# Layer 1 of a two-layer decoder trunk: the order of five engines taken from a list scheduler in the kernel's source, in place of the framework's order on four of them

## The chip, the cores and the metric

The kernel runs on one core of one Trainium2 chip. The metric is the device time of one execution in microseconds, as the median of several runs. One profiled execution gives the trace from which all other figures come.

## What is computed

A trunk of two layers over 1024 tokens of width 1024, batch 1. Layer 0 mixes by gated causal pooling; then one K/V pair is made from the stream; layer 1 is attention with 16 query heads on 2 shared K/V heads, in a window of 128 tokens, with a bias by distance and a sink per head. The part that the change touches, cut from the reference:

```python
kb, vb = shared_kv_blocks(x, c_act, ...)     # rmsnorm, modulate, x @ w_kv, banded blocks
h = modulate(rmsnorm(x, norm_g[l]), shift, scale)
q, z = jnp.split(h @ w_in, 2, axis=-1)
s = jnp.einsum('bqhgd,bkhd->bhgqk', qn, kn) + pos_bias
s = jnp.where(mn, s, NEG_INF)
m = jnp.maximum(jnp.max(s, axis=-1, keepdims=True), sink)
p = jnp.exp(s - m)
p = p / (jnp.sum(p, axis=-1, keepdims=True) + jnp.exp(sink - m))
o = jnp.einsum('bhgqk,bkhd->bqhgd', p, vn)
y = (o * jax.nn.silu(z)) @ w_out
x = x + gate[:, None, :] * y
return rmsnorm(x, final_g)
```

## The kernel before

Activations lie transposed: channels on the 128 partitions, tokens along the free axis. The stream is eight tiles `xk[n]` of 128 channels x 1024 tokens. The 1024 tokens are worked in two halves of 512, q=0 and q=1. Every matrix product is made of three passes of half precision each (fp32r): high times high, high times low, low times high. So every operand exists as a high part and a low part: ScalarE (ACT) casts the high part, VectorE (DVE) subtracts it from the value to get the low part. A **dense step** is the three matmuls of one slice of 128 channels (L200 to L202), and a dense tile has eight of them, or four for a tile of the output product.

Layer 1 (L1022 to L1414, from about 603 us on) is a list `specs` of pieces, worked one after the other: for each half and each group r of four heads a `project` (two tiles of queries L1085, two of gates L1102); keys and values of the second half (L1047, L1063); the output product in parts (`out_part` L1199, and in quarters of 256 tokens at the very end, `out_quarter` L1222); the norms' statistics and the final norm (`finish` L1277). Pieces marked `bare` only start other work and add 0.1 to the clock.

Between the steps of these pieces run the **attention blocks** (`attend` L1119), one per head group and block of 128 tokens, 32 in all. A block's chain crosses four engines: PE makes the scores (L1138, L1139, tile ps_S); DVE masks (L1140) and takes row maxima (L1144); ACT takes four exponentials (L1148, tile pt); DVE the reciprocal (L1151) and the division pt (L1152); PE transposes pt (L1158, tile ps_tp); ACT and DVE split that into high and low (L1161, L1162); POOL masks it with two selects (L1167, L1170); PE multiplies with the values (L1181, L1182, tile ps_o); ACT and DVE add, gate and split the result into qt (L1184 to L1194). `LAGS`, `GAPS` and `FIRST` date the blocks' three pieces on PE, in a clock that counts only dense steps (KSTEP, L1038).

`Modulated` (L924) makes the normed and modulated input of a product, tile hm: DVE makes xn from x (L937), ACT adds the shift and casts the high part (L939), DVE takes the low part (L943). hk1 is the input of the second half's keys and values, h11 that of its queries and gates; `prepare` (L1348) dates their eight steps each.

**Weights.** `load_any` (L1251) fetches a weight two pieces ahead and splits it in the same place of the program. A weight that the first half has split already comes back from memory on POOL's queue (L1262, tiles kw). A new one is loaded on SP's queue into raw1, of which there are two (L1265), cast by ACT (L1266) and split by DVE (L1267), and its two parts are stored to memory by SP (`keep`, L147). The four last output weights (tile wo) stay on the chip and are not stored.

**What sets the order.** Only PE's instructions are issued in the order written (`manual_schedule`, L1401). The order of ACT, DVE, POOL and SP comes from the framework's own scheduler, which sees the same program.

Of the kernel before, what the change touches and what calls it, by code (L numbers as in the profile page):

```python
# [59 lines left out]
def trunk(ctx, tc, xT, c, pack, ada_first, ada_rest, wu0_in, wg0_in, wa, wg, wao, wkv,  # L60
# [976 lines left out]

    KSTEP = 3 * 0.2133  # L1038

    def gemm_steps(w, off, acts, n, done, cols=H):  # L1040
        ps = bank("d")[:, :cols]
        for k in range(n):
            dense_mm(ps, w, off, acts, k, n)
            yield KSTEP * cols / H
        done(ps)

    def keys(q, hk, ps=None):  # L1047
        def done(ps):
            cols = half(q)
            for kv in range(2):  # L1050
                a, b = slice(kv * 64, kv * 64 + 64), slice((1 - kv) * 64, (1 - kv) * 64 + 64)
                nc.scalar.copy(out=KH[kv][a, cols], in_=ps[a, :])
                nc.scalar.copy(out=KH[kv][b, cols], in_=ps[a, :])
                hs = KH[kv][a, cols].bitcast(F32)
                nc.vector.tensor_sub(out=KL[kv][a, cols], in0=ps[a, :], in1=hs)
                nc.vector.tensor_sub(out=KL[kv][b, cols], in0=ps[a, :], in1=hs)
# [6 lines left out]
    def values(q, hk, ps=None):  # L1063
        def done(ps):
            vts[q] = bp.tile([P, H], F32, tag="ol", name="vt", bufs=1)
            nc.scalar.copy(out=vts[q], in_=ps)
# [4 lines left out]
    def values_split(q):  # L1071
        def run(w):
            ps = bank("d")
            for j in range(4):
                nc.tensor.transpose(ps[:, j * P:(j + 1) * P], vts[q][:, j * P:(j + 1) * P], ident)
            pv = ps.rearrange("p (s c) -> p s c", c=64)
            vh, vl = VS[:, q * 8:q * 8 + 8, 0, :], VS[:, q * 8:q * 8 + 8, 1, :]
            nc.scalar.copy(out=vh, in_=pv)
            nc.vector.tensor_sub(out=vl, in0=pv, in1=vh.bitcast(F32))
# [5 lines left out]
    def queries(q, r, j, h1):  # L1085
        def run(w):
            if j == 0:
                pool, tag, bufs = (bp, "q2", 2) if r < 2 else (hp, "h", 8)
                qts[q, r] = pool.tile([P, 2, 2, H], F32R, tag=tag, name="qt", bufs=bufs)
            qt = qts[q, r]  # L1090

            def done(ps):
                for e in range(2):
                    a, b = slice(e * 64, e * 64 + 64), slice((1 - e) * 64, (1 - e) * 64 + 64)
                    nc.scalar.activation(qt[a, j, e, :], ps[a, :], AF.Copy, scale=0.125)
                    nc.vector.scalar_tensor_tensor(
                        out=qt[b, j, e, :], in0=ps[a, :], scalar=0.125,
                        in1=qt[a, j, e, :].bitcast(F32), op0=ALU.mult, op1=ALU.subtract)
# [3 lines left out]
    def gates(q, r, j, h1):  # L1102
        def run(w):
            if j == 0:
                szs[q, r, "tile"] = bp.tile([P, 2, H], F32, tag="szb", name="szb", bufs=2)
            sz = szs[q, r, "tile"]

            def done(ps):
                nc.scalar.activation(sz[:, j, :], ps, AF.Tanh, scale=0.5)
                nc.vector.scalar_tensor_tensor(out=sz[:, j, :], in0=sz[:, j, :], scalar=1.0,  # L1110
                                               in1=ps, op0=ALU.add, op1=ALU.mult)
# [7 lines left out]
    def attend(q, r, b):  # L1119
        kv = r // 2  # L1120
        qt = qts[q, r]
        cols = slice((b % 4) * P, (b % 4) * P + P)


        pt = bp.tile([P, 4, P + 8], F32, tag="P", name="pt", bufs=2)
        nc.gpsimd.tensor_copy(out=pt[:, :, P:P + 1],
                              in_=nsink[:, 4 * r:4 * r + 4].unsqueeze(2))
        nm = sp.tile([P, 4], F32, tag="nm", name="nm")
        den = sp.tile([P, 4], F32, tag="den", name="den")
        for j in range(2):  # L1130
            s = bank("S").rearrange("p (e c) -> p e c", e=2)
            lo = 0 if b else P
            if b == 0:
                nc.vector.memset(s[:, :, :P], NEG)
            for e in range(2):
                lhs = qt[:, j, e, cols]
                ks = slice((b - 1) * P + lo, (b + 1) * P)
                mm(s[:, e, lo:], lhs, KH[kv][:, ks], start=True, stop=False)  # L1138
                mm(s[:, e, lo:], lhs, KL[kv][:, ks], start=False, stop=True)  # L1139
            nc.vector.copy_predicated(out=s[:, :, :P], mask=tri, data=s[:, :, P:])  # L1140
            for e in range(2):
                i = 2 * j + e
                hd = 4 * r + i
                nc.vector.tensor_tensor_reduce(  # L1144
                    out=pt[:, i, :P], in0=s[:, e, :P], in1=bias[:, hd, :],
                    scale=-1.0, scalar=nsink[:, hd:hd + 1], op0=ALU.add, op1=ALU.min,
                    accum_out=nm[:, i:i + 1])
                nc.scalar.activation(pt[:, i, :P + 1], pt[:, i, :P + 1], AF.Exp,  # L1148
                                     bias=nm[:, i:i + 1], scale=-1.0,
                                     accum_out=den[:, i:i + 1])  # L1150
        nc.vector.reciprocal(out=den, in_=den)  # L1151
        nc.vector.tensor_mul(out=pt[:, :, :P], in0=pt[:, :, :P],  # L1152
                             in1=den.unsqueeze(2).broadcast_to([P, 4, P]))
        yield LAGS[0]
        tp = bank("tp")
        for j in range(2):
            for e in range(2):
                nc.tensor.transpose(tp[:, (e * 2 + j) * P:(e * 2 + j + 1) * P],  # L1158
                                    pt[:, 2 * j + e, :P], ident)
# [310 lines left out]
```

## Time and profile before

| | us |
|---|---|
| median of three runs | 984.7 (983.31 to 985.41) |
| the profiled execution, its own time | 985.74 |
| its span (first to last instruction in the trace) | 983.9 |
| granted TensorE clock, mean of the span | 0.992 |

| engine | busy us | share | instructions |
|---|---|---|---|
| PE (matmul) | 964.3 | 98% | 4538 |
| DVE | 748.7 | 76% | 1405 |
| ACT | 421.5 | 43% | 860 |
| POOL | 152.9 | 16% | 238 |

The span lies 1.84 us below the execution's own time. A row of the trace's timeline has the start, the length, the engine, the line, the operation, the tiles (out<-in) and, in brackets, how long the engine had stood idle before it and what ended that idle time. PE's matmuls overlap, so the distance from one start to the next, not the length, is what one costs.

### The profile page before, as it was taken

How to read it: one execution, taken by the hardware profiler on the slowest of the kernel's cores; microseconds unless marked ns; L12 is line 12 of the kernel's file. 1: busy time of each engine (PE TensorE's matmuls, PEld its weight loads, DVE VectorE, ACT ScalarE, POOL GpSimd, SP SyncE). 2: the span in 40 equal slices, each digit the busy share in tenths (PEclk: the TensorE clock that was granted, in tenths of full speed). 3: DMA queues.
4: the chain of work that ended last, by engine and by line, in shares of the span. 5: the costliest groups of instructions: out<-in, count | busy, mean ns of one | idle time of the engine just before them, and what ended most of it. 6: DMA issues, size and time to landing. Idle time of an engine off the chain costs nothing.

```text
span 983.9 us, 12776 instructions
## 1 busy us (share of the span) xinstructions
PE 964.3 (98%) x4538; PEld 804.2 (82%) x4538; DVE 748.7 (76%) x1405; ACT 421.5 (43%) x860; POOL 152.9 (16%) x238
## 2 busy tenths in 40 slices
PE   8999999999999999999999999999999999999996
PEld 6788888888888888888888888887888888887896
DVE  5897978686977799676765478498999666777684
ACT  5534434332433344551122245355665434454434
POOL 3100000000000000000022101231313433443523
PEclk9999999999999999999999999999999999999998
DMA  9452621254225411788878726745556454353022
GB/s 337 167 183 107 203 97 65 76 202 150 65 81 197 150 64 57 258 280 307 303 277 276 273 65 225 275 138 182 207 207 221 130 171 141 131 185 101 1 87 86
DMA packets 51570, 165.53 MB, mean 168 GB/s; under 512 B 5681, under 2 KB 7857, under 8 KB 51378
## 3 DMA queue, kind: packets, MB, share of 16 engines
q1 hardware_dynamic: 39120, 119.10, 34.8%
q0 software_dynamic: 12240, 44.57, 13.4%
q10 hardware_dynamic: 146, 1.05, 0.4%
q8 instruction: 35, 0.57, 0.2%
q14 instruction: 29, 0.24, 0.1%
HBM read 128.00 MB, written 36.70 MB: 167 GB/s over the span
## 4 chain that ended last, share of the span: by engine, by line
PE 80%; DVE 14%; ACT 2%; issue 2%; DMA 1%; POOL 1%; POOLq 0%; DVEq 0%; SPq 0%; ACTq 0%
PE ps_d L211 14%; PE ps_S L211 9%; PE ps_d L633 9%; PE ps_d L200 7%; PE ps_d L201 7%; PE ps_d L202 7%; PE ps_S L633 4%; PE ps_o L211 4%; PE ps_tp L211 3%; PE ps_d L371 2%; PE ps_o L633 2%; PE ps_tp L633 2%; DVE tmp L539 2%; PE ps_tp L1158 1%; PE ps_S L1139 1%
## 5 line engine op out<-in xcount | busy, mean ns | idle before, releaser
L201 PE MATMUL ps_d<-hm,w 128*128 128x512 f32 x264 | 103.4, 392 | 1.9 <-DVE hm L943 1.9
L200 PE MATMUL ps_d<-hm,w 128*128 128x512 f32 x264 | 104.7, 397 | 0.0
L202 PE MATMUL ps_d<-hm,w 128*128 128x512 f32 x264 | 103.4, 392 | 0.0
L236 DVE CUSTOM_DVE_ANT_0 tmp<-tmp,cact,pk 128x1024 f32<-128x1024 f32 x48 | 60.7, 1282 | 28.2 <-DMA tmp<-ada_rest 27.9
L211 PE MATMUL ps_d<-gh,wh 128*128 128x512 f32 x224 | 81.9, 389 | 0.0
L1148 ACT ACTIVATE pt<-pt,nm 128x129 f32<-128x129 f32 x128 | 50.2, 395 | 36.9 <-DVE nm L1144 33.0
L211 PE MATMUL ps_S<-gh,wh 128*128 128x512 f32 x192 | 64.5, 390 | 0.0
L633 PE MATMUL ps_d<-hs,ws 128*128 128x512 f32 x264 | 63.4, 389 | 0.0
L201 PEld LDWEIGHTS ps_d<-hm,w 128*128 128x128 f32 x264 | 49.8, 189 | 11.4 <-DVE hm L943 2.3
L202 PEld LDWEIGHTS ps_d<-hm,w 128*128 128x128 f32 x264 | 49.7, 188 | 11.1 <-DMA w<-kw 0.4
L633 PEld LDWEIGHTS ps_d<-hs,ws 128*128 128x128 f32 x264 | 49.6, 188 | 10.3
L200 PEld LDWEIGHTS ps_d<-hm,w 128*128 128x128 f32 x264 | 49.8, 189 | 9.2
L539 DVE TENSOR_TENSOR tmp<-tmp 128x1039 f32<-128x1039 f32 (+3 forms) x40 | 49.4, 1234 | 6.8 <-ACT tmp L669 5.8
L531 POOL MEMSET tmp<- 128x16 f32 x16 | 1.7, 112 | 331.4 <-DVE tmp L539 117.9
L633 PE MATMUL ps_d<-ha,ws 128*128 128x512 f32 x216 | 51.9, 389 | 0.0
L126 ACT CAST wh<-raw 128x1024 fp32r<-128x1024 f32 x28 | 29.4, 1050 | 49.4 <-PE ps_d L211 33.9
L609 ACT CAST ws<-tw 128x512 fp32r<-128x512 f32 x44 | 26.7, 621 | 53.7 <-PE ps_tp L211 15.1
L211 PEld LDWEIGHTS ps_d<-gh,wh 128*128 128x128 f32 x224 | 42.0, 188 | 8.8
L633 PEld LDWEIGHTS ps_d<-ha,ws 128*128 128x128 f32 x216 | 40.6, 188 | 8.4
L1262 POOL DMA_DIRECT2D w<-kw x58 | 31.5, 544 | 85.1 <-PE ps_d L202 44.5
L211 PE MATMUL ps_d<-gh,wl 128*128 128x512 f32 x112 | 43.6, 389 | 0.0
L1188 DVE SCALAR_TENSOR_TENSOR of<-ps_o,ol 64x256 f32<-64x256 f32 x64 | 26.6, 416 | 20.9 <-ACT ol L1184 20.2
(308 smaller groups left out, 2569.6 us busy)
## 6 DMA issues: line engine op xcount, KB each, us to landing
w<-kw POOLq DMA_DIRECT2D x58, 512.0 KB, 4.2
tmp<-ada_rest SPq DMA_DIRECT2D x42, 512.0 KB, 4.8
raw<-wa SPq DMA_DIRECT2D x28, 512.0 KB, 3.5
kw<-w SPq DMA_DIRECT2D x24, 512.0 KB, 2.8
raw<-wao SPq DMA_DIRECT2D x20, 512.0 KB, 5.3
ad<-ada_first SPq DMA_DIRECT2D x16, 512.0 KB, 4.7
x<-xT SPq DMA_DIRECT2D x32, 256.0 KB, 5.9
kept_g<-tmp SPq DMA_DIRECT2D x14, 512.0 KB, 2.9
```

The costliest lines, as they stand in the source:

```text
L126: nc.scalar.copy(out=wh, in_=raw)
L200: mm(ps, lh, acts(k, 0), start=k == 0, stop=False)
L201: mm(ps, lh, acts(k, 1), start=False, stop=False)
L202: mm(ps, ll, acts(k, 0), start=False, stop=k == n - 1)
L211: mm(p, lhs, acts(k, hl, q), start=start and k == 0 and s == 0, stop=stop and k == n - 1 and s == 2)
L236: nc.vector.tensor_tensor_reduce(out=raw, in0=raw, in1=ca, scale=0.5, scalar=pk[:, bcol:bcol + 1], op0=ALU.mult, op1=ALU.add, accum_out=ad ...
L539: nc.vector.tensor_add(out=nx[:, 2 * s - 1:], in0=cur[:, 2 * s - 1:], in1=cur[:, s - 1:PAD + T - s])
L609: nc.scalar.copy(out=ws[i][:, 0, :], in_=src)
L633: mm(ps, lhs, acts(k, hl), start=start and k == 0 and s == 0, stop=k == 3 and s == 2, skip_group_check=True)
L1148: nc.scalar.activation(pt[:, i, :P + 1], pt[:, i, :P + 1], AF.Exp, bias=nm[:, i:i + 1], scale=-1.0, accum_out=den[:, i:i + 1])
L1188: nc.vector.scalar_tensor_tensor(out=of[e * 64:(e + 1) * 64, :], in0=o[0:64, es], scalar=0.5, in1=ol[0:64, es], op0=ALU.mult, op1=ALU.add)
L1262: nc.gpsimd.dma_start(dst, src)
```

## The change

No operation of layer 1 is added or taken away (`Modulated` becomes `Second` there, with the same three operations per step). What changes is who decides the order. Every operation is first noted with its engine, a length in us estimated by the author, and the tiles (and parts of tiles) that it reads and writes. Objects `Buf` stand for tiles that are not yet allocated, with the ring of buffers that each takes its turn in. `in_order` then plans. PE's notes keep the order in which they are written. Each gets a wanted time from the lengths ahead of it on PE. The notes of the other engines get theirs backward from those who need them. Then a simulated run takes, at each step, the engine that can begin earliest, and on it the ready note with the smallest wanted time. All notes are issued in the order of their planned beginnings, under a manual schedule of all five engines (PE, ACT, DVE, POOL, SP).

Beside that, `load_any` is parted in two: `fetch_any` issues the load two pieces ahead, `split_any` takes the cast, the split and the stores one piece ahead. Three added `bare` entries hand large buffers on, and each adds 0.1 to the clock of the blocks.

The diff, cut to its core:

```diff
     KSTEP = 3 * 0.2133
+    class Buf:
+        def __init__(self, make, ring=None, turns=0):
+            self.make, self.tile, self.touched, self.parts = make, None, [], {}
...
+    LAG = {PE: 0.25, ACT: 0.15, DVE: 0.12, POOL: 0.12, SP: 0.0}
+
+    def note(engine, length, f, reads=(), writes=(), lag=None):
...
+    def in_order():
...
+            if n.engine == PE:
+                n.want = t
+                t += n.length
+        for n in reversed(notes):
+            if n.engine != PE:
+                n.want = min([t + 12.0] + [
+                    m.want if n in m.follows and n not in m.needs
+                    else m.want - n.length - n.lag for m in n.next])
...
+                if some:
+                    begin = max(free[e], min(n.ready for n in some))
+                    n = min((n for n in some if n.ready <= begin),
+                            key=lambda n: (n.want, number[n]))
+                    if best is None or begin < best[0]:
+                        best = begin, n
...
+        return sorted(notes, key=lambda n: (n.begin, number[n]))
...
+        note(PE, 0.69 if cols == H else 0.365, f,
+             w[0].on + w[1].on + a[0].on + a[1].on, [(ps, 0)])
...
-                nc.scalar.activation(pt[:, i, :P + 1], pt[:, i, :P + 1], AF.Exp,
-                                     bias=nm[:, i:i + 1], scale=-1.0,
-                                     accum_out=den[:, i:i + 1])
-        nc.vector.reciprocal(out=den, in_=den)
...
+            note(ACT, 0.41, lambda: nc.scalar.activation(
+                pt()[:, i, :P + 1], pt()[:, i, :P + 1], AF.Exp, bias=nm()[:, i:i + 1],
+                scale=-1.0, accum_out=den()[:, i:i + 1]),
+                [(nm, i), (pt, "sink")], [(pt, i), (den, i)])
...
+        note(DVE, 0.66, lambda: nc.vector.tensor_mul(
+            out=pt()[:, :, :P], in0=pt()[:, :, :P],
+            in1=den().unsqueeze(2).broadcast_to([P, 4, P])),
+            [(den, i) for i in rows], [(pt, i) for i in rows])
...
-    def load_any(key):
...
+    def fetch_any(key):
...
+                note(POOL, 0.55, lambda: nc.gpsimd.dma_start(w[i](), kept_w[key][i]),
+                     kept_at[key][i].on if key in kept_at else (), w[i].on, 5.0)
...
+        raw = tile_of("raw1", bp, [P, 1024], F32, 2)
+        src = (wb if key[0] == "b" else wbo)[key[1:]]
+        note(SP, 0.35, lambda: nc.sync.dma_start(raw(), src), (), [(raw, 0)], 3.6)
+        return key, raw, None
+
+    def split_any(key, raw, w):
...
+        note(ACT, 1.0, lambda: nc.scalar.copy(out=w[0](), in_=raw()), [(raw, 0)], w[0].on)
+        note(DVE, 1.16, lambda: nc.vector.tensor_sub(
+            out=w[1](), in0=raw(), in1=w[0]().bitcast(F32)), [(raw, 0)] + w[0].on, w[1].on)
...
+                note(SP, 0.35, lambda: nc.sync.dma_start(kept_w[key][i], w[i]().bitcast(F32)),
+                     w[i].on, kept_at[key][i].on, 4.0)
...
-    hk1 = Modulated(1, None, 8, 48)
-    h11 = Modulated(1, None, 16, 24)
...
+            note(DVE, 0.68, lambda: nc.vector.scalar_tensor_tensor(
+                out=f(), in0=xk[k][:, half(1)], scalar=a, in1=rb(), op0=ALU.mult, op1=ALU.mult),
+                x_on(k, 1) + [(rb, 0)], [(f, 0)])
...
+    hk1, h11 = Second(8, 48), Second(16, 24)
...
-        keys(1, hk1), values(1, hk1),
+        keys(1, hk1), values(1, hk1), bare(lambda: large.extend(hk1.tiles)),
...
-    with tc.manual_schedule(engines={mybir.EngineType.PE}):
...
+    loaded = {srcs[0]: [whole(rings[t][1]) for t in ("wh", "wl")]}
+    asked = [fetch_any(specs[i][0]) for i in srcs[1:2]]
...
+                loaded[srcs[nxt]] = split_any(*asked.pop(0))
+            if nxt + 1 < len(srcs):
+                asked.append(fetch_any(specs[srcs[nxt + 1]][0]))
...
+    with tc.manual_schedule(engines=set(LAG)):
+        for n in in_order():
+            n.f()
```

**ScalarE at the last output weights.** These are the rows of ACT around the third and fourth of the weights that stay (wo), where the third block of the last head group is under way. In the program before (cur is the high part of the transposed block, szb the gate, ol and qt the block's result):

```order
L1161 CAST cur<-ps_tp 128x512
L1184 ACTIVATE ol<-ps_o 64x512
L1266 CAST wo<-raw_7576 128x1024
L1193 CAST qt<-of 128x2x128
L1148 ACTIVATE pt,den<-pt,nm 128x129 x2
L1109 ACTIVATE szb<-ps_d 128x512
L1266 CAST wo<-raw_7664 128x1024
L1148 ACTIVATE pt,den<-pt,nm 128x129 x2
L1184 ACTIVATE ol<-ps_o 64x512
```

and the same place now (P is the tile that was called pt, ph that of cur):

```order
L1364 CAST ph<-ps_tp 128x512
L1397 ACTIVATE ol<-ps_o 64x512
L1341 ACTIVATE P,den<-P,nm 128x129 x4
L1288 ACTIVATE szb<-ps_d 128x512
L1413 CAST qt<-of 128x2x128
L1534 CAST wo<-raw_7452 128x1024
L1534 CAST wo<-raw_7471 128x1024
```

Of the two casts of wo that stood between and ahead of the exponentials, both now follow them, behind the gate and the block's qt.

**VectorE at the eighth tile of hk1.** These are the rows of DVE ahead of the eighth low part of hk1 (hm). Before, from the gating of one block to the division of the next:

```order
L1144 ISA pt,nm<-ps_S,bias,nsink 128x128
L1144 ISA nm 128x1
L1110 SCALAR_TENSOR_TENSOR szb<-szb,ps_d 128x512
L1267 TENSOR_TENSOR w_5308<-raw_5309,w_5307 128x1024
L1151 RECIPROCAL den<-den 128x4
L943 SCALAR_TENSOR_TENSOR hm<-xn,adac,hm 128x512
L1152 TENSOR_TENSOR pt<-pt,den 128x4x128
```

and now, from the division of the block ahead, which the three last hm of hk1 follow:

```order
L1350 TENSOR_TENSOR P<-P,den 128x4x128
L1660 SCALAR_TENSOR_TENSOR hm<-xn,adac,hm 128x512 x3
L1410 TENSOR_TENSOR of<-of,szb 128x256
L1321 MEMSET ps_S 128x2x128
L1290 SCALAR_TENSOR_TENSOR szb<-szb,ps_d 128x512
L1415 TENSOR_TENSOR q_4850<-of,q_4850 128x2x128
L1654 SCALAR_TENSOR_TENSOR xn<-x,acol,rb_5035 128x512
L1403 SCALAR_TENSOR_TENSOR of<-ps_o,ol 64x256
L1365 TENSOR_TENSOR ph<-ps_tp,ph 128x512
L1330 COPY_PREDICATED ps_S<-tri,ps_S 128x2x128 x2
L1403 SCALAR_TENSOR_TENSOR of<-ps_o,ol 64x256
```

The eighth hm stood behind the maxima, a gate (szb) and the split of the first new weight. It now stands ahead of the gate and of all that the next block needs (the maxima follow the last row shown, and that split follows the maxima).

**SyncE between the loads and stores of new weights.** The rows of SP for the first of them, before (raw is the tile loaded, kw the copy in memory):

```order
L1265 DMA raw_5356<-wb 128x1024
L147 DMA kw<-w_5307 128x1024
L147 DMA kw<-w_5308 128x1024
L1265 DMA raw_5440<-wb 128x1024
L147 DMA kw<-w_5354 128x1024
L147 DMA kw<-w_5355 128x1024
```

and now (raw, wh and wl behind kw<- are the names that the two split parts have there):

```order
L1518 DMA raw_4804<-wb 128x1024
L1542 DMA kw<-raw 128x1024
L1518 DMA raw_5362<-wb 128x1024
L1542 DMA kw<-raw 128x1024
L1542 DMA kw<-wh 128x1024
L1518 DMA raw_5414<-wb 128x1024
L1542 DMA kw<-wl 128x1024
```

The next load stood behind both stores of a weight; it now stands between the two.

More of the change, by code (lines that the diff above doesn't have):

```diff
@@ L1038, in trunk, with __call__ @@
     KSTEP = 3 * 0.2133
+    PE, ACT, DVE, POOL, SP = ET.PE, ET.Activation, ET.DVE, ET.Pool, ET.SP
+    notes, touched = [], {}
+    class Buf:
+        def __init__(self, make, ring=None, turns=0):
+            self.make, self.tile, self.touched, self.parts = make, None, [], {}
+            self.old = self.before = None
+            if ring is not None:
+                self.old = ring[-turns] if len(ring) >= turns else None
+                self.before = ring[-1] if ring else None
+                ring.append(self)
+        def __call__(self):
+            if self.tile is None:
+                self.tile = self.make()
+            return self.tile
@@ new lines, in trunk, with there, ring_of, tile_of @@
+    rings = {}
+    def there(tile):
+        return Buf(lambda: tile)
+    def ring_of(name, *tiles):
+        rings[name] = [there(t) for t in tiles]
+    def tile_of(name, pool, shape, dtype, bufs):
+        return Buf(lambda: pool.tile(shape, dtype, tag=name, name=name, bufs=bufs),
+                   rings.setdefault(name, []), bufs)
+    large = [Buf(lambda t=t: t) for t in (*hk0.tiles, *h10.tiles)]
+    first_tiles, large = large[4:], large[:4]
+    def large_tile(shape, name):
+        t = Buf(lambda: hp.tile(shape, F32R, tag="h", name=name))
+        t.old = large.pop(0)
+        return t
@@ L1121, in attend @@
         qt = qts[q, r]
[L1122 to L1131, printed above, removed]
+        c = b % 4
+        cols = slice(c * P, c * P + P)
@@ new lines, in attend, with scores @@
+        pt = tile_of("P", bp, [P, 4, P + 8], F32, 2)
+        nm, den = [tile_of(t, sp, [P, 4], F32, 2) for t in ("nm", "den")]
+        note(POOL, 0.25, lambda: nc.gpsimd.tensor_copy(
+            out=pt()[:, :, P:P + 1], in_=nsink[:, 4 * r:4 * r + 4].unsqueeze(2)),
+            (), [(pt, "sink")])
+        ks = slice((b - 1) * P if b else 0, (b + 1) * P)
+        k_on = [(t, (h, x)) for t in (KHb[kv], KLb[kv]) for h in range(2)
+                for x in sorted({max(b - 1, 0) // 4, b // 4})]
+        def scores(j):
+            bk = bank_of("S")
+            s = lambda: bk().rearrange("p (e c) -> p e c", e=2)
@@ L1151, in attend @@
-        nc.vector.reciprocal(out=den, in_=den)
-        nc.vector.tensor_mul(out=pt[:, :, :P], in0=pt[:, :, :P],
-                             in1=den.unsqueeze(2).broadcast_to([P, 4, P]))
-        yield LAGS[0]
[L1155 to L1159, printed above, removed]
-        cur = bp.tile([P, 2, H], F32R, tag="ph", name="cur", bufs=2)
@@ L1211, in out_part @@
+            for i in range(2):
+                yield from tile(i, 2 * n2 + i)
         return ("o", part, n2), run
@@ new lines, in split_any, with note_stats, sums, f @@
+        return w
+    def note_stats(sq, n, more=None):
+        st = bank_of("o")
+        v, rs = [tile_of(t, sp, [P, 8], F32, 2) for t in ("v", "rs")]
+        parts = (sq,) if more is None else (sq, more)
+        def sums(i, t):
+            def f():
+                for j in range(n):
+                    mm(st()[:, j:j + 1], t()[:, j * P:(j + 1) * P], invd,
+                       start=i == 0 and j == 0, stop=j == n - 1 and i == len(parts) - 1)
+            note(PE, 0.15 * n, f, t.on, [(st, 0)])
+        for i, t in enumerate(parts):
+            sums(i, t)
+        note(DVE, 0.2, lambda: nc.vector.tensor_scalar_add(
+            out=v()[:, :n], in0=st()[:, :n], scalar1=EPS), [(st, 0)], [(v, 0)])
+        note(POOL, 1.0, lambda: nc.gpsimd.tensor_tensor(
+            out=rs()[:, :n], in0=v()[:, :n], in1=mhalf[:, :n], op=ALU.pow), [(v, 0)], [(rs, 0)])
+        state["rs"] = rs
@@ L1389, in trunk @@
         *project(1, 2, h11, GAPS[6]),
[L1390 removed]
+        *project(1, 3, h11, GAPS[7]), bare(lambda: large.extend(h11.tiles)),
         *project_out(1, 0)[:2],
```

497 lines of the change are left out of this document (350 added, 147 removed).

## The prediction

> **What bounds the kernel now.** I read the page first (busy times and the chain), then who waited for whom on the matrix engine from 570 us on, then the timeline at each wait that this names, and last the busy times by stretch.
>
> ```profile
> span 983.9 us, 12776 instructions
> PE 964.3 (98%) x4538; PEld 804.2 (82%) x4538; DVE 748.7 (76%) x1405; ACT 421.5 (43%) x860; POOL 152.9 (16%) x238
> PE 80%; DVE 14%; ACT 2%; issue 2%; DMA 1%; POOL 1%; POOLq 0%; DVEq 0%; SPq 0%; ACTq 0%
> ```
>
> TensorE (PE) is busy for 964.3 of 983.9 us, and the chain that ended last is mostly PE. The change removes no matmul. So all it can win is time in which PE stands still or runs slowly while layer 1 is computed (from about 603 us on). The waits view of PE from 570 us lists all of it (total, times, longest):
>
> ```profile
> PE ps_tp L1158 <- DVE pt L1152: 3.4, 5, 2.0
> PE ps_d L201 <- DVE hm L943: 1.9, 1, 1.9
> PE ps_tp L173 <- POOL rs L166: 1.1, 1, 1.1
> PE ps_o L161 <- DVE sqq L1243: 0.6, 1, 0.6
> PE ps_o L161 <- ACT sqq L1241: 0.2, 1, 0.2
> ```
>
> The last three lie behind the last big matmul (973 us) and belong to the closing chain of the norm. The first two are six stalls in the middle; the timeline of PE gives them one by one (start, length, then in brackets the idle time before it):
>
> ```profile
> 664.45 0.63 PE L1158 MATMUL ps_tp<-ident,pt 128*128 128x128 f32 x4 [0.24 <-DVE pt L1152]
> 673.63 0.50 PE L201 MATMUL ps_d<-hm,w 128*128 128x512 f32 x1 [1.91 <-DVE hm L943]
> 687.78 0.63 PE L1158 MATMUL ps_tp<-ident,pt 128*128 128x128 f32 x4 [0.17 <-DVE pt L1152]
> 734.84 0.63 PE L1158 MATMUL ps_tp<-ident,pt 128*128 128x128 f32 x4 [0.52 <-DVE pt L1152]
> 744.61 0.63 PE L1158 MATMUL ps_tp<-ident,pt 128*128 128x128 f32 x4 [0.45 <-DVE pt L1152]
> 892.90 0.74 PE L1158 MATMUL ps_tp<-ident,pt 128*128 128x128 f32 x4 [1.97 <-DVE pt L1152]
> ```
>
> They sum to 5.3 us. The stretches (busy us of PE, PEld, DVE, ACT, POOL with counts, then the granted clock, DMA share, GB/s) show what else they cost, and who is short of time:
>
> ```profile
> 640.00:660.00 20.00, 20.00 (x102) 16.86 (x101) 19.70 (x43) 12.48 (x26) 6.50 (x10) 1.00 0.34 113
> 660.00:670.00 10.00, 9.76 (x50) 7.96 (x49) 9.72 (x27) 5.44 (x14) 3.36 (x5) 1.00 0.38 116
> 670.00:680.00 10.00, 8.09 (x34) 6.32 (x33) 9.36 (x22) 5.54 (x15) 1.18 (x2) 0.83 0.74 258
> 680.00:760.00 80.00, 78.86 (x395) 65.86 (x395) 74.32 (x192) 49.76 (x125) 18.41 (x22) 1.00 0.56 204
> 760.00:880.00 120.00, 120.00 (x599) 101.35 (x598) 80.62 (x238) 53.73 (x163) 48.10 (x70) 1.00 0.45 149
> 890.00:900.00 10.00, 8.03 (x35) 6.65 (x34) 7.58 (x22) 4.09 (x16) 3.67 (x5) 0.83 0.15 47
> 900.00:973.00 73.00, 73.00 (x452) 65.53 (x451) 52.35 (x128) 34.22 (x88) 28.92 (x29) 1.00 0.13 48
> ```
>
> Two things are to be seen. Behind each of the two long stalls the granted clock is 0.83 over 10 us, so 10 x 0.17 = 1.7 us more are lost each time; the four short ones (0.17 to 0.52) leave it at 1.00. And from 640 to 760 us VectorE (DVE) is busy for 113 of 120 us: there it is nearly the bound, and the order of its work decides whether PE's piece is ready. After 760 us it has a third of its time free (80.6 of 120).
>
> The Trainium skill (TensorE: Matmul & The Clock Gate, HAM oscillation) says that PE falls to half clock after idle gaps of more than about 3.4 us. This trace differs: gaps of 1.91 and 1.97 us already brought it. By that rule both stalls would cost their idle time alone, and what there is to win would be 3.4 us less; the measured clock decides.
>
> **The ceiling.** 5.3 us of idle and 2 x 1.7 us of clock make 8.7 us. PE's starts show a little more, since a stalled matmul also loses the overlap with its neighbour (0.1 to 0.16 us at each of six): 9.5 us at most.
>
> **Part 1, ScalarE's written order at the last weights (the stall at 892.90).** The rows of the transfer queue, ScalarE (ACT) and VectorE that lead to it:
>
> ```profile
> 881.90 1.69 SPq L1265 DMA_DIRECT2D raw<-wbo  x2
> 886.36 1.05 ACT L1266 CAST wo<-raw 128x1024 fp32r<-128x1024 f32 x1 [3.28 <-DMA raw<-wbo]
> 887.62 0.40 ACT L1148 ACTIVATE pt<-pt,nm 128x129 f32<-128x129 f32 x1
> 889.02 1.04 ACT L1266 CAST wo<-raw 128x1024 fp32r<-128x1024 f32 x1
> 890.35 0.39 ACT L1148 ACTIVATE pt<-pt,nm 128x129 f32<-128x129 f32 x1
> 890.96 1.19 DVE L1267 TENSOR_TENSOR wo<-raw,wo 128x1024 fp32r<-128x1024 f32 x1
> 892.07 0.69 DVE L1152 TENSOR_TENSOR pt<-pt,den 128x512 f32<-128x512 f32 x1
> ```
>
> ACT stood for 3.28 us at the cast of the third output weight, whose transfer was still under way; the four exponentials of the block stood behind it, two of them even behind the fourth cast, and on DVE the fourth split (1.19) stood between the reciprocal and the division pt. In the new rows all four exponentials stand ahead of the third cast, and DVE's reciprocal and division are neighbours. Without the cast ahead of them the exponentials follow their maxima, so the last ends more than 2 us sooner. 1.97 + 1.7 = 3.7 us go. What is late next there is nothing that I can find: the third and fourth weight are used two output tiles later, and their casts (2 x 1.05) and splits (2 x 1.19) fit before the next block's maxima, as before.
>
> **Part 2, VectorE's order ahead of the second-half keys (the stall at 673.63).** PE waits for the low half of the eighth modulated tile of hk1. DVE's rows:
>
> ```profile
> 664.81 1.99 DVE L937 SCALAR_TENSOR_TENSOR xn<-x,acol,rb 128x512 f32<-128x512 f32 x3
> 671.04 0.68 DVE L1110 SCALAR_TENSOR_TENSOR szb<-szb,ps_d 128x512 f32<-128x512 f32 x1
> 671.64 1.21 DVE L1267 TENSOR_TENSOR w<-raw,w 128x1024 fp32r<-128x1024 f32 x1
> 672.86 0.71 DVE L943 SCALAR_TENSOR_TENSOR hm<-xn,adac,hm 128x512 fp32r<-128x512 f32 x1
> 673.50 0.68 DVE L1152 TENSOR_TENSOR pt<-pt,den 128x512 f32<-128x512 f32 x1
> ```
>
> What PE needs next of these, from its timeline (the transposes of that division, and the first step with h11):
>
> ```profile
> 677.93 0.75 PE L1158 MATMUL ps_tp<-ident,pt 128*128 128x128 f32 x4
> 781.77 0.48 PE L200 MATMUL ps_d<-hm,w 128*128 128x512 f32 x1
> ```
>
> At 664.81 DVE began tiles of xn that only h11 needs (used from 781.77 us on), and just ahead of the wanted hm it evacuated a gate and split a weight that comes a whole weight tile later: 0.68 + 1.21 us at the head of the queue. In the new rows the eighth hm stands one attention block earlier, ahead of that block's maxima. The work moved behind it (one gate, one split, one xn) is wanted later than the keys. 1.91 + 1.7 = 3.6 us go. DVE is full here, so the price is that something else is later; the nearest is the division pt of the same block, done at 674.2 and wanted at 677.93 in the old order, some 3.6 us sooner once the stall is gone. I count nothing for it, between 0 and the 0.52 of the next short stall.
>
> **Part 3, the four short stalls (0.24 + 0.17 + 0.52 + 0.45 = 1.4 us).** All are the division pt, late behind other DVE work. The new order puts reciprocal and division next to each other in every block, but often an hm, a split or evacuations just ahead of them, where the exponentials leave a hole. Bounds: 1.4 us won, or 1.4 us and as much again lost, because with the two long stalls gone PE arrives up to 7 us sooner at the same full DVE; but h11's work can wait until 781.77 us, and DVE has some 6 us unused between 640 and 760. I take 0.
>
> **Part 4, what moves without a price.** SP now issues the next raw load between the two stores of a split weight, 0.3 to 0.4 us earlier; only that second store waits behind it, and nobody reads it for tens of us. POOL's row is nearly the same. Three added steps of the program, each 0.1 on the clock by which the attention blocks are dated, shift some blocks by one step of three matmuls on PE; nothing is added. Waits of split weights come one weight later in the program, but the same rings (raw1 x2, three pairs) free them at the same matmuls. In the closing chain all five rows are the same, so its time stays:
>
> ```profile
> 975.64 0.70 POOL L166 TENSOR_TENSOR rs<-v,mhalf 128x2 f32<-128x2 f32 x1 [1.26 <-DVE v L164]
> 977.65 2.74 DVE L1295 TENSOR_TENSOR x<-x,ps_tp 128x256 f32<-128x256 f32 x8 [2.09 <-PE ps_tp L173]
> ```
>
> **The sum.** 3.7 + 3.6 + 0 = 7.3 us. The profiled execution took 985.74 us, 1.84 beyond its span; it would come to 978.4. The median of the three runs, 984.7, lies 1.0 below it: **977.4 us**.
>
> **The rivals.** One: only the ACT stall goes, and VectorE stays late from 640 to 760. For it: 113 of 120 us busy, and a plan with one length per operation meets operations whose length varies:
>
> ```profile
> L1152 DVE TENSOR_TENSOR pt<-pt,den x32: 668/692/1504, 630.6 to 938.5; 128x512 f32<-128x512 f32 x32
> DMA to landing us min/median/max: 3.8/4.4/14.1
> ```
>
> (the first is the division, shortest, median, longest; the second is the raw loads of L1265). The plan gives the division 0.66 us. Against it: the eighth hm is moved by a whole block, far more than 0.8. Time: 984.7 - 3.7 = 981.0. The Trainium skill (SBUF — State Buffer, Who interferes with whom) says that a VectorE instruction with two SBUF inputs contends with a GpSimd instruction that reads SBUF. The division of 1.50 us began while a select of POOL ran, so the trace agrees; a plan that knows only engines would meet this at random.
>
> Two, it does not do what it says: each stall that goes comes back elsewhere in the same full stretch, and a new cast or split stands in front of another block: 984.7.
>
> Three, slower: the weight casts. The plan counts 0.35 + 3.6 us from issue to landing, the trace's median is 4.4 and the longest 14.1. Sixteen fresh weights come through here, and each cast now has a fixed place in ACT's row with exponentials behind it. A cast that waits as the one at 886.36 did costs 3.7 us. Two of them undo the gain, from the third on it is slower: 977.4 + 3 x 3.7 = 988.5. Against it: in the old order, also fixed, only one of sixteen waited, and the load is now issued no later.
>
> **How the numbers follow.** Forecast 0.66, rival one 0.15, two 0.08, three 0.11. This kernel's measurement tells 0.2% (2 us) from no change. The forecast and rival one are faster: 0.81; rival two is the same: 0.08; three is slower: 0.11. The forecast's own range is 975.2 (the 9.5 us ceiling) to 979.5 (short stalls lose another 1.4 and some); taking in rival one with 2 us for a stall that comes back gives 975.0 to 983.0, which leaves out rivals two and three, 0.19.
>
> **What would show it.** In the new profile: no PE wait for hm (L1660) and no ACT wait for a raw output weight ahead of exponentials; granted clock 1.00 in every 10 us from 640 to 970; PE's waits for the division under 1.5 us in total; a closing chain of the same 10 to 11 us. Wrong if PE waits anew for a weight, a modulated tile or an exponential by more than 2 us in one place, or if the clock falls again.

## The result, and the profile after

| | before | after |
|---|---|---|
| median, us (6 runs each) | 985.06 (983.31 to 986.08) | 975.49 (975.02 to 977.02) |
| the profiled execution / its span, us | 985.74 / 983.9 | 977.02 / 975.3 |
| PE waits from 570 us to the last big matmul, us | 5.3, six stalls | 0.65, one |

The ratio is 0.9909 (95% interval 0.9896 to 0.9922), some 9 us. The prediction was 977.4, within 975.0 to 983.0; the result lies 1.9 us below the forecast, near the lower end. The profiled execution after is the slowest of its six. The page and the waits of PE from 570 us on (total, times, longest):

```profile
span 975.3 us, 12806 instructions
PE 961.7 (99%) x4538; PEld 803.7 (82%) x4538; DVE 751.3 (77%) x1405; ACT 421.1 (43%) x860; POOL 149.4 (15%) x238
```

```profile
PE ps_tp L1574 <- POOL rs L1564: 1.1, 1, 1.1
PE ps_tp L1360 <- DVE P L1350: 0.6, 1, 0.6
PE ps_o L1557 <- DVE ol L1487: 0.6, 1, 0.6
PE ps_o L1557 <- ACT ol L1484: 0.2, 1, 0.2
```

The wait for hm is gone, and of five waits for the division one is left; the other three rows are the closing chain. The same stretches as before (busy us of PE, PEld, DVE, ACT, POOL, then the granted clock):

```profile
640.00:660.00 20.00, 20.00 (x101) 16.86 (x101) 18.90 (x43) 12.44 (x30) 5.47 (x9) 1.00 0.40 135
660.00:670.00 10.00, 10.00 (x52) 8.40 (x51) 9.75 (x27) 5.83 (x16) 4.51 (x7) 1.00 0.43 148
670.00:680.00 10.00, 10.00 (x52) 8.42 (x51) 9.92 (x29) 7.93 (x22) 1.55 (x2) 1.00 0.68 195
680.00:760.00 80.00, 79.35 (x402) 66.77 (x401) 77.28 (x191) 49.90 (x126) 18.11 (x23) 1.00 0.64 221
890.00:900.00 10.00, 10.00 (x51) 8.47 (x50) 7.43 (x25) 5.48 (x20) 5.58 (x8) 1.00 0.31 105
```

The clock is 1.00 in all of them. VectorE is busier than before: 18.90 + 9.75 + 9.92 + 77.28 = 115.9 of 120 us, against 113.1. It does its work with one wait of PE left, of 0.65 us. The two old places, from DVE's and PE's timelines, first the eighth hm, then the division of the block at the third kept weight:

```profile
662.53 0.69 DVE L1350 TENSOR_TENSOR P<-P,den 128x512 f32<-128x512 f32 x1
663.14 2.07 DVE L1660 SCALAR_TENSOR_TENSOR hm<-xn,adac,hm 128x512 fp32r<-128x512 f32 x3
672.19 0.39 PE L1191 MATMUL ps_d<-hm,wh 128*128 128x512 f32 x1
882.92 0.69 DVE L1350 TENSOR_TENSOR P<-P,den 128x512 f32<-128x512 f32 x1
886.78 0.60 PE L1360 MATMUL ps_tp<-ident,P 128*128 128x128 f32 x4
```

The eighth hm is done at 665.2 and wanted at 672.19, by the second matmul of the eighth step; the division is done at 883.6 and wanted at 886.78.

**The account of the profiled pair.** These are starts of PE and its stretch of the chain that ends layer 0, before and after, and the last big matmul:

```profile
589.48 10.88 PE ps_S L211 x48
973.02 0.28 PE L202 MATMUL ps_d<-qt,wo 128*128 128x256 f32 x1
```

```profile
590.67 10.88 PE ps_S L211 x48
965.31 0.28 PE L1192 MATMUL ps_d<-qt,wo 128*128 128x256 f32 x1
```

Layer 0, in which no instruction differs, took 1.2 us more. Layer 1 went from 383.54 to 374.64, 8.9 us less. The closing chain went from 983.9 - 973.02 = 10.9 to 975.3 - 965.31 = 10.0. That makes 1.2 - 8.9 - 0.9 = -8.6, the difference of the spans.

To price each stall I summed what PE's starts lie apart beyond the usual pitch (227 ns for a matmul of 512 columns, 120 for 256, 109 for 128); this takes in the idle time, the half clock behind it and the lost overlap. Before: 3.81 us around 673.63, 3.74 around 892.90, and 0.35 + 0.37 + 0.71 + 0.60 = 2.03 at the four short stalls. After: 0.76 at the one that is left (712.83). That is 3.81 + 3.74 + 2.03 - 0.76 = 8.8 us, against the 8.9 that layer 1 became shorter.

### The profile page after: what moved, and what is told of

Same layout as the page of the kernel before. It is cut to its first block, busy times and chain, and to the rows that moved or that the text cites. A ratio compares the mean times of both kernels' runs of the same rounds, so it can differ in the third digit from the quotient of the medians.

```text
span 975.3 us, 12806 instructions
## 1 busy us (share of the span) xinstructions
PE 961.7 (99%) x4538; PEld 803.7 (82%) x4538; DVE 751.3 (77%) x1405; ACT 421.1 (43%) x860; POOL 149.4 (15%) x238
## 4 chain that ended last, share of the span: by engine, by line
PE 86%; DVE 10%; issue 2%; DMA 1%; POOL 1%; ACT 1%; POOLq 0%; SPq 0%; DVEq 0%; ACTq 0%
PE ps_d L211 14%; PE ps_S L211 9%; PE ps_d L633 9%; PE ps_d L1190 7%; PE ps_d L1192 7%; PE ps_d L1191 7%; PE ps_S L633 4%; PE ps_o L211 4%; PE ps_tp L211 3%; PE ps_d L371 2%; PE ps_o L633 2%; PE ps_tp L633 2%; DVE tmp L539 2%; PE ps_d L304 2%; PE ps_S L304 1%
## 5 line engine op out<-in xcount | busy, mean ns | idle before, releaser
L1341 ACT ACTIVATE P<-P,nm 128x129 f32<-128x129 f32 x128 | 50.2, 394 | 46.7 <-DVE nm L1337 46.5
L1190 PE MATMUL ps_d<-hm,wh 128*128 128x512 f32 x176 | 69.5, 395 | 0.0
L1191 PE MATMUL ps_d<-hm,wh 128*128 128x512 f32 x176 | 68.7, 390 | 0.0
L1192 PE MATMUL ps_d<-hm,wl 128*128 128x512 f32 x176 | 68.6, 390 | 0.0
L211 PEld LDWEIGHTS ps_S<-gh,wh 128*128 128x128 f32 x192 | 35.9, 188 | 7.4
L1372 POOL TENSOR_SCALAR_AFFINE_SELECT pp<-ph 128x1024 fp32r<-128x1024 f32 x28 | 30.8, 1098 | 57.9 <-DVE ph L1365 57.8
L128 DVE TENSOR_TENSOR wl<-raw,wh 128x1024 fp32r<-128x1024 f32 x28 | 34.2, 1221 | 6.6 <-ACT wh L126 5.2
L1192 PEld LDWEIGHTS ps_d<-hm,wl 128*128 128x128 f32 x176 | 33.0, 188 | 7.1
```

What stands on the lines that cost most here:

```text
L128: nc.vector.tensor_sub(out=wl, in0=raw, in1=wh.bitcast(F32))
L211: mm(p, lhs, acts(k, hl, q), start=start and k == 0 and s == 0, stop=stop and k == n - 1 and s == 2)
L1190: mm(p, lh, a[0](), start=k == 0, stop=False)
L1191: mm(p, lh, a[1](), start=False, stop=False)
L1192: mm(p, ll, a[0](), start=False, stop=k == n - 1)
L1341: note(ACT, 0.41, lambda: nc.scalar.activation(pt()[:, i, :P + 1], pt()[:, i, :P + 1], AF.Exp, bias=nm()[:, i:i + 1], scale=-1.0, accum_ou ...
```

## The experiments

Each kernel was run beside the kernel before, so the ratio to it (95% interval) is what compares them: the changed kernel has 0.9909.

**All but the plan.** The notes are issued in the order noted, only PE's order is fixed. PE's instructions stand exactly as in the changed kernel.

```diff
-    with tc.manual_schedule(engines=set(LAG)):
-        for n in in_order():
+    with tc.manual_schedule(engines={PE}):
+        for n in notes:
```

> The changed kernel without the planner: all notes are issued as noted, with PE's order exactly as in the changed kernel, and the order of ScalarE, VectorE, GpSimd and SyncE left to the framework as before. Loads two weights ahead, splits one ahead, and the three added steps of 0.1 stay. Theory (the planned order of the other engines is the whole gain): 983 to 985, with the two long stalls back at the eighth hm and at the third kept weight. Rival (the splitting one weight later, or the shift of attention blocks on PE by a step, is what removed the stalls): 975 to 977.

986.29 us, ratio 1.0011 (0.9996 to 1.0026): the whole gain is gone. The stalls of PE in this kernel's timeline:

```profile
688.12 0.63 PE L1360 MATMUL ps_tp<-ident,P 128*128 128x128 f32 x4 [2.28 <-DVE P L1350]
718.07 0.63 PE L1360 MATMUL ps_tp<-ident,P 128*128 128x128 f32 x4 [2.17 <-DVE P L1350]
894.40 0.63 PE L1360 MATMUL ps_tp<-ident,P 128*128 128x128 f32 x4 [1.27 <-DVE P L1350]
```

The last is at the old place, the block of the third kept weight. At the other old place, the eighth hm, PE waits 0.70 us (at 673.42). The two longest stalls, of over 2 us, are at blocks that waited 0.17 us and not at all before, so the places came out only in part as I expected. The splits one weight later and the shifted blocks do not take the stalls away. The planned order is the gain, in some form.

**The plan, held on fewer engines.** Three kernels take the planned list and fix PE and VectorE, PE and ScalarE, or PE alone; the framework orders the rest, and does change it.

```diff
-    with tc.manual_schedule(engines=set(LAG)):
+    with tc.manual_schedule(engines={PE, DVE}):     # {PE, ACT}; {PE}
```

> The changed kernel with the planned order fixed on PE and VectorE alone; ScalarE, GpSimd and SyncE are ordered by the framework again from the planned list. Theory (the gain is VectorE's order, the engine that is 94 to 98% busy there): 975 to 977.5, no stall of PE of 1.5 us or more. Rival (ScalarE's order, with exponentials ahead of casts, carries it): a stall of 1.5 us or more comes back, 979 or above.

> The changed kernel with the planned order fixed on PE and ScalarE alone; VectorE, GpSimd and SyncE are ordered by the framework from the planned list. Theory (VectorE's order is the gain): stalls at the divisions come back, 3 us or more in all, 979 to 983. Rival (ScalarE's order carries it): 975 to 977.5.

> The changed kernel with only PE's order fixed, as before the change; the instructions are handed to the framework in the planned order, and it may reorder the other four engines, which it does (some 250 places on ScalarE, 460 on VectorE). Theory now, after the runs with only VectorE or only ScalarE fixed came within 1 to 2 us of the full change (what counts is that the instructions reach the framework in the order of planned beginnings, not that it is held to it): 975.5 to 978, no stall of 1.5 us or more. Rival (at least one of the two busy engines has to be held to the plan): stalls of 2 us come back, 980 to 986, as when the notes were handed over in the order noted (986.3).

977.54 us, 0.9930 (0.9909 to 0.9951); 976.49, 0.9918 (0.9897 to 0.9940); 978.16, 0.9941 (0.9921 to 0.9962). So VectorE need not be held, nor ScalarE, against my theory that it was VectorE's order; with neither held, most of the gain is still there. What remained with PE alone fixed is a wait for the values' high part on ScalarE and two for the division:

```profile
PE ps_o L1390 <- ACT VS L1247: 1.2, 1, 1.2
PE ps_tp L1360 <- DVE P L1350: 0.7, 2, 0.4
```

From 1.0011 to 0.9941 (6.9 us of 984.5) is the order in which instructions are handed over, and from 0.9941 to 0.9909 (some 3 us, and the intervals just touch) is holding the engines to it.

**All held, with no plan.**

```diff
-        for n in in_order():
+        for n in notes:
```

> The changed kernel with all five engines fixed, but in the order in which the notes are written, with no planning. Theory (holding the engines to an order brings nothing by itself; a block's maxima, reciprocal and division then stand together on VectorE, which must stand still for the four exponentials at each block): slower than before; worked out, 1.5 us at each of the 13 blocks of the full stretch, less the 6 us that VectorE had free there: 13 x 1.5 - 6 = 13 us, so about 998, between 990 and 1010. Rival (the fixed order is what helps, whichever it is): 976 to 982.

1078.31 us, 1.0960 (1.0941 to 1.0978): slower by 94 us, where I expected 13. The longest row of the waits of DVE, ACT, POOL and PE:

```profile
DVE den L1348 <- ACT P L1341: 50.6, 32, 2.7
```

```profile
ACT P L1341 <- POOL P L1309: 74.2, 23, 3.6
```

```profile
POOL pp L1372 <- DVE ph L1365: 251.1, 27, 30.1
```

```profile
PE ps_S L1326 <- DVE ps_S L1321: 23.4, 7, 6.0
```

These waits are totals over layer 1. The wait at the reciprocal was sized rightly (50.6 / 32 = 1.6 us a block, I had 1.5). What I left out is that a block's chain then crosses all queues in lockstep: its copy of the sinks (L1309) stands on POOL behind selects (L1372) that wait for their input, so the exponentials wait some 3 us more (74.2 / 23). Part of the loss is the clock: it stands at one half for 75 us in all between 600 and 1070 us, which is at most 37 of the 94 us. Holding an order brings nothing by itself.

**How right the lengths must be.** One number of the plan, then all of them:

```diff
-        note(SP, 0.35, lambda: nc.sync.dma_start(raw(), src), (), [(raw, 0)], 3.6)
+        note(SP, 0.35, lambda: nc.sync.dma_start(raw(), src), (), [(raw, 0)], 0.5)
```

> The changed kernel with one number of the plan changed: a raw load is taken to land 0.5 us after its issue instead of 3.6. The planner then puts the third kept weight's cast ahead of all four exponentials of the block under way, and its split ahead of that block's division; the rest of the plan stays as it is. The third rival of the prediction (a cast that waits for its landing at the head of ScalarE's row costs 3.7 us): PE waits 2 us at the transposes, 977.5 to 979.2. Theory now, worked out from the trace of the changed kernel: the load lands at about 882.2, the exponentials end at 885.0 instead of 882.5 and the division at 885.9, and PE wants it at about 886.9, so nothing waits: 975.5.

976.42 us, 0.9919 (0.9900 to 0.9939), not to be told from the changed kernel. The third cast stands at the head of ACT's row and waits, and PE goes through (no idle time ahead of its row). The cast's row names PE, but its load was issued at 877.5 us and loads took some 4.1 us there, so it waited for the load:

```profile
881.51 1.05 ACT L1534 CAST wo<-raw 128x1024 fp32r<-128x1024 f32 x1 [2.87 <-PE ps_d L1192]
884.36 0.69 DVE L1350 TENSOR_TENSOR P<-P,den 128x512 f32<-128x512 f32 x1
886.35 0.60 PE L1360 MATMUL ps_tp<-ident,P 128*128 128x128 f32 x4
```

The prediction's third rival priced such a cast at 3.7 us; here it costs nothing, since the division is still done 1.3 us ahead.

```diff
-            self.engine, self.length, self.f = engine, length, f
+            self.engine, self.length, self.f = engine, length if engine == PE else 0.6, f
```

> The changed kernel with every planned length off PE set to 0.6 us (the plan has 0.2 to 1.4 there); lags and PE's lengths stay. Theory (the lengths need not be right to a few tenths, since PE comes for each tile some us after it is ready): within 3 us of the changed kernel, 975.5 to 978.5. Rival (the lengths carry the gain; a row of maxima planned at twice its length pushes what follows out of its hole): two or more stalls of over 1 us come back, 979 to 985.

987.57 us, 1.0036 (1.0018 to 1.0055): slower than the kernel before, so my theory falls. A stall at a division is back, at another block than before. The low part of h11 is 0.37 us late for four steps in a row, of which two are shown, and one block's masked half comes 1.3 us late from GpSimd:

```profile
678.26 0.72 PE L1360 MATMUL ps_tp<-ident,P 128*128 128x128 f32 x4 [2.12 <-DVE P L1350]
776.97 0.50 PE L1191 MATMUL ps_d<-hm,raw 128*128 128x512 f32 x1 [0.37 <-DVE hm L1660]
778.29 0.51 PE L1191 MATMUL ps_d<-hm,raw 128*128 128x512 f32 x1 [0.36 <-DVE hm L1660]
```

One landing wrong by 3.1 us is forgiven; lengths wrong throughout are not.

**Part 1 undone.** In the first run only the casts and splits went back; the second puts the rows of both engines back word for word.

```diff
 ACT:  -exp, exp, exp, exp, gate, qt, cast 3, cast 4
       +cast 3, qt, exp, exp, gate, cast 4, exp, exp
 DVE:  -max x4, of x2, of*sz, reciprocal, division, gate, qt, x, split 3, split 4
       +of x2, of*sz, max x2, split 3, qt, max x2, gate, x, reciprocal, split 4, division
```

> The changed kernel with part 1 undone alone: the casts of the third and fourth kept output weight stand again ahead of and between the four exponentials of the block under way, their splits again among its maxima and behind its reciprocal, as in the order before. All else is in the new order. My theory (the order on ScalarE made the stall): the third cast waits for its load, the exponentials behind it are 2 us or more late, PE waits 1.5 to 2.1 us at the transposes of that block and then runs at a granted clock of about 0.83 over 10 us: 975.5 + 3.7 = 979.2. Rival (the load of that weight lands early enough now, so its place no longer matters): no wait of PE over 0.3 us there, 975.5.

> The changed kernel with the rows of ScalarE and VectorE around the third and fourth kept weight (one block's worth) put back word for word into the order of before: third cast, two exponentials, gate, fourth cast, two exponentials; third split among the maxima, fourth split between reciprocal and division. Nothing else moves, and the list of instructions keeps its order otherwise. Theory (that order made the stall, whatever else was late): PE waits 1.7 to 2.1 us at the transposes of that block, and loses another 1.7 us in those executions where the clock falls behind it: 977.4 to 979.3. Rival (the earlier run with the casts alone ahead waited only 1.0 us, so the rest of the old stall came from VectorE being late already): 1.0 us at most, 976.5.

The first gave 981.45 us, 0.9962 (0.9949 to 0.9975), but it carries a second change that I had not meant (below), so only its waits are read: 0.99 us at this place. The second gave 978.99 us, 0.9942 (0.9925 to 0.9960), some 3 us more than the changed kernel:

```profile
882.35 1.05 ACT L1571 CAST wo<-raw 128x1024 fp32r<-128x1024 f32 x1 [2.86 <-DMA raw<-wbo]
886.95 1.19 DVE L1572 TENSOR_TENSOR wo<-raw,wo 128x1024 fp32r<-128x1024 f32 x1
888.06 0.69 DVE L1386 TENSOR_TENSOR P<-P,den 128x512 f32<-128x512 f32 x1
888.89 0.63 PE L1397 MATMUL ps_tp<-ident,P 128*128 128x128 f32 x4 [1.55 <-DVE P L1386]
```

The stall is back, smaller by 0.4 us than before. The late load alone does not make it (0 with the third cast ahead of all four exponentials, in the run above). What this run has beyond that is the third split among the maxima, the fourth cast among the exponentials and the fourth split (1.19 us) ahead of the division; they were not tried one by one. The block is the third of the third head group of this half; the words above its rows in the section on the change call that group the last, which is wrong.

**Part 2 undone, and a stall made on purpose.** The eighth low part of hk1 goes back behind the next block's reciprocal, or three instructions behind its division.

```diff
 DVE:  -division, hm 6, hm 7, hm 8, ..., max x4, split, reciprocal, division, of*sz, gate, xn
       +division, hm 6, hm 7, ..., max x4, split, reciprocal, hm 8, division, of*sz, gate, xn
  or   +division, hm 6, hm 7, ..., max x4, split, reciprocal, division, of*sz, gate, xn, hm 8
```

> The changed kernel with part 2 undone as it was worded: the eighth low part of hk1 stands again behind the next block's maxima, its gate, the split of the first new weight and the reciprocal, ahead of the division. Theory of the prediction (the place behind that block is what made the stall of 1.91 us): PE waits 1.9 us for hm and loses 1.7 us of clock, 979.1. Rival (it was the whole of VectorE's queue that was late, by the three xn for h11 and the rest; in the new order VectorE comes to that place about 2 us sooner, so even there hm is ready when PE wants it at 672.87): a wait of 0.3 us at most, 975.5.

> The changed kernel with the eighth low part of hk1 put three instructions behind the next block's division, so that VectorE ends it at about 674.9, when PE wants it at 672.87. Theory: PE waits about 2.1 us, and the granted clock falls to about 0.83 over the next 10 us, as behind the stalls of 1.91 and 1.97 us before: 975.5 + 2.1 + 1.7 = 979.3. Rival (a stall costs its idle time alone, and the low clock behind the old ones came of something else): 977.6, clock 1.00.

978.38 us, 0.9930 (0.9915 to 0.9945), and 982.20, 0.9975 (0.9961 to 0.9990). In the first, PE does not wait for hm at all, but with little to spare: the low part is done at 669.26, and the second matmul of the eighth step, which needs it, starts at 669.55:

```profile
668.54 0.72 DVE L1689 SCALAR_TENSOR_TENSOR hm<-xn,adac,hm 128x512 fp32r<-128x512 f32 x1
669.55 0.39 PE L1218 MATMUL ps_d<-hm,wh 128*128 128x512 f32 x1
```

The 672.87 at which both expectations let PE want it in the changed kernel is a step of the next tile; it is 672.19. So the old place alone did not make the old stall: VectorE came to it at 672.86 before and at 668.54 here, 4.3 us sooner, while PE came only 2.0 us sooner (it would have come at some 671.56 before). This run's extra 2 to 3 us came from the unmeant change. My way of moving one note had also rewritten the list between engines, so that the clearing of ps_S stood behind the scores that go into the other half of the same bank; the framework then made it wait for them, and the second clearing, which stands behind a split, made PE wait. The two runs that moved rows and kept the planned list between engines (the rows put back above, the split moved below) have no such wait. The rows:

```profile
702.18 0.27 DVE L1348 MEMSET ps_S<- 128x256 f32 x1 [1.90 <-PE ps_S L1354]
704.04 0.30 PE L1353 MATMUL ps_S<-KH,qt 128*128 128x128 f32 x1 [1.99 <-DVE ps_S L1348]
```

The run with the eighth hm further behind has both stalls, which answers the question of the clock:

```profile
672.21 0.50 PE L1220 MATMUL ps_d<-hm,wh 128*128 128x512 f32 x1 [1.94 <-DVE hm L1691]
706.44 0.30 PE L1355 MATMUL ps_S<-KH,qt 128*128 128x128 f32 x1 [1.99 <-DVE ps_S L1350]
```

```profile
670.00:680.00 10.00, 8.06 (x42) 6.62 (x41) 7.87 (x21) 6.44 (x14) 0.20 (x1) 1.00 0.81 262
700.00:710.00 10.00, 8.01 (x38) 6.64 (x38) 7.57 (x18) 4.08 (x11) 0.47 (x2) 0.90 0.31 97
710.00:720.00 10.00, 10.00 (x49) 8.30 (x48) 9.97 (x21) 4.91 (x13) 4.22 (x3) 0.93 0.75 248
```

Of two stalls of nearly the same length the first left the clock at 1.00 and the second lowered it. Theory and rival are each right once.

**The stall that is left.** DVE and POOL ahead of it in the changed kernel:

```profile
709.02 1.10 POOL L1372 TENSOR_SCALAR_AFFINE_SELECT pp<-ph 128x1024 fp32r<-128x1024 f32 x1 [2.92 <-DVE ph L1365]
709.40 1.79 DVE L1535 TENSOR_TENSOR wl<-raw,wh 128x1024 fp32r<-128x1024 f32 x1
710.19 1.96 POOL L1376 TENSOR_SCALAR_AFFINE_SELECT ph<-ph 128x1024 fp32r<-128x1024 f32 x1
711.32 1.37 DVE L1350 TENSOR_TENSOR P<-P,den 128x512 f32<-128x512 f32 x1
712.83 0.63 PE L1360 MATMUL ps_tp<-ident,P 128*128 128x128 f32 x4 [0.65 <-DVE P L1350]
```

The split takes 1.79 us where its usual is 1.22, the division 1.37 where its usual is 0.69, and the second select 1.96 against 1.10 of the first. Of the 32 divisions in this trace, the thirty that ran beside no select took 0.69 to 0.70 us and the two that ran beside one 1.37 us. One instruction was moved:

```diff
 DVE:  -max x4, split, reciprocal, division, of*sz
       +max x4, reciprocal, division, split, of*sz
```

> The changed kernel with one instruction moved: the split of the weight that stood ahead of the reciprocal of the block whose division PE still waits for (0.65 us) is put behind that division. In the trace of the changed kernel that split took 1.79 us instead of 1.21 and the division 1.37 instead of 0.69, while GpSimd's two selects ran. Theory (those two slowed operations in a row are the stall): the reciprocal starts when the exponentials end, even a division of 1.37 us is done before PE comes, no wait there, 0.8 us less: 974.7. Rival (VectorE is full, so the split moved behind makes the next thing late): 975.5 or more, with a new wait within 10 us of that place.

975.03 us, 0.9911 (0.9895 to 0.9926): no difference that can be measured, though the wait is gone:

```profile
707.83 1.44 DVE L1379 TENSOR_TENSOR P<-P,den 128x512 f32<-128x512 f32 x1
709.19 1.21 DVE L1565 TENSOR_TENSOR wl<-raw,wh 128x1024 fp32r<-128x1024 f32 x1
709.44 0.60 PE L1390 MATMUL ps_tp<-ident,P 128*128 128x128 f32 x4
728.74 0.63 PE L1390 MATMUL ps_tp<-ident,P 128*128 128x128 f32 x4 [0.16 <-DVE P L1379]
```

The division is still slow beside the selects, now with room for it; a wait of 0.16 us comes 19 us later. No version beats the changed kernel by more than can be told.

## Why the prediction was right, point by point

- **Part 1** (3.7 us): 3.74 by PE's starts. With the old rows put back, the stall came back with 1.55 us of idle time.
- **Part 2** (3.6 us): 3.81. The size holds, the reason only in part: the place "one attention block earlier" was not needed, as the run with the old place shows, though that left 0.3 us to spare where the new place leaves 7.0. VectorE came to the old place earlier too, in the new order of the rest of its work; which part of that order counted most was not tried.
- **Part 3** (taken as 0, bounds 1.4 won or lost): 2.03 before, 0.76 after, 1.3 us won, which is most of the 1.9 us by which the result lies below the forecast. This is the term that was mis-sized, and with it VectorE's role: busier than before, it is late only once, and there beside GpSimd's selects. (The first step with h11 in the profile before is at 770.71 us; the 781.77 that the prediction names is in its second tile, so there was 11 us less room than it says.) The Trainium skill (SBUF — State Buffer, Who interferes with whom) says that a VectorE instruction with two inputs in SBUF contends with a GpSimd instruction that reads SBUF; the split (1.79 us), the division (1.37) and the select (1.96) beside them agree.
- **The clock term** (1.7 us behind each stall of 2 us) is right in size and wrong as a certainty: of nine stalls of 1.9 to 2.3 us in layer 1 (all kernels but the one held without a plan), five were followed by a lower clock in the profile (both of before; 706.46 in the first run of part 1, 1.99 us long; 678.26 and 706.44 above) and four were not (672.21 and 704.04 above, and both of over 2 us in the kernel without the plan). The Trainium skill (TensorE: Matmul & The Clock Gate, HAM oscillation) sets its rule at gaps of over about 3.4 us; five gaps of about 2 us here contradict it, and four agree. What decided it is in the last section: where the stall falls. In the profile before both fell the costly way, so that the term came in full is luck of that execution; with no stall of that length there is nothing to lose, but another execution of before may not have lost these 3.4 us.
- **The closing chain** (unchanged) ended 0.9 us sooner, with the same instructions. Of that 0.5 is at the last four transposes, which ran at half clock before (1.26 us from their start to the first addition that follows) and at the full clock after (0.75): the clock fell at 975.2 us, ahead of them, before, and at 970.6 us, behind them, after. The other 0.4 is between the end of the last addition and the end of the output (3.5 and 3.1 us), and its cause stays open. Neither is shown to come from the change.
- **The rivals.** One (981.0) did not come: VectorE was not late. Two (984.7) is what the same program does without the plan. Three (988.5) was tried on its own at one place: the cast that waits for its load costs nothing there.

## What to carry to other kernels

When an engine is 95% busy and PE still waits for it, look at what it does just before the late piece, not at how fast it is; here the order of work was worth 9 us, and VectorE did no less of it. A list scheduler in the source pays through the dates it gives, even where the framework may still reorder, and its lengths have to be near the measured ones; a fixed order without dates was 94 us slower. Two halves of one bank are one tile to the framework, which adds the waits: an instruction moved in the list can wait for what it does not use.

## What the runs showed of the hardware that was not expected

Whether a stall of 2 us brings the half clock depends on when it comes, even with the same instructions. In each of the fourteen traces (one per kernel) the recorded clock changes only on a grid of 3.413 us, and the grid lies differently in each execution. In all but the kernel held without a plan, each recorded low stretch ahead of the closing chain is one step of that grid: 3.41 us at half clock, which is the 1.7 us lost. Of the nine stalls above, the five with a low clock behind them fell into one step, four whole and one (706.44) with 1.83 of its 1.99 us, and the next step was the low one. The four without lay across a border of two steps, with at most 1.25 (704.04), 1.74 (672.21), 1.25 (688.12) and 1.91 us (718.07) in one of them. The 1.83 and the 1.91 overlap, so the idle time within a step tells nearly all, but not all.

The first stretches of the program, in which nothing differs, show the same (before, then after, then the low step after):

```profile
10.00:20.00 10.00, 9.96 (x39) 6.72 (x38) 7.67 (x9) 7.44 (x12) 2.98 (x2) 1.00 1.04 409
```

```profile
10.00:20.00 10.00, 10.00 (x30) 6.75 (x30) 6.75 (x7) 6.48 (x11) 2.06 (x2) 0.83 1.04 409
14.91:18.32 3.41, 3.41 (x9) 2.65 (x9) 3.20 (x5) 3.41 (x7) 1.28 (x1) 0.50 1.04 410
```

PE is not idle ahead of that low step. What stands there is four matmuls that read a single row of 512 (L430). After, they run from 12.48 to 14.46 us, all within the step from 11.50 to 14.91; before, they run from 11.57 to 13.54, across a border at 12.64. In seven of the fourteen traces the four lie within one step, and these are the seven in which the next step is low. So idle time alone is not what counts. What does was not tried; no run changed those matmuls.

The 1.2 us that layer 0 took longer in the profile after come of this start. At first the matmuls of 512 columns lie 427 ns apart, twice the usual 227, until 9.2 us before and 11.5 us after. So PE is 0.9 us behind at those four matmuls, and 2.5 us once the low step is over; 1.3 us of that are made up where PE waits less than before. Low steps also fit the spread of the kernel before: of its 13 executions in the last comparison the three fastest (982.1 to 982.3 us) have a mean clock of 0.996 to 0.998, the next five (982.6 to 983.8) 0.994, and the five slowest (985.3 to 986.0) 0.992 to 0.994.
